# gMLP projections in two passes, with Strassen's algorithm for u and g

## The chip, the cores and the metric

The kernel runs on one core of a Trainium2 chip. The metric is the device time of one execution in microseconds: 1731.4 us is the median of three runs of the kernel before (1731.1 to 1732.46). The trace shown below is one more execution, recorded by the hardware profiler.

## The reference

One layer of a hybrid encoder, sequence 4096, width 1024, everything in float32. With `h = RMSNorm(x) * norm_gain * (1 + scale) + shift`:

```
q, k, v, g_attn, u, v_gm, g_gm = split(h @ w_in)        # 512,128,128,512,512,512,512 columns
A  = windowed_GQA(q, k, v) * silu(g_attn)               # 128-token blocks, +-128 tokens
vn = rms(v_gm in 8 groups of 64)                        # per token and group
sv = einsum('gts,bcsge->bctge', w_s, vn) + b_s          # mixing inside each 128-token chunk
M  = u * sv * silu(g_gm)
out = x + gate * (concat[A, M] @ w_out)
```

shift, scale and gate come from `silu(c) @ w_ada + b_ada`. The norm gain and scale are folded into the weights per input row (`gcol`), the shift into a bias row (`bias1`, `bias2`), and the token's 1/rms (`rstd`) is multiplied in when a product leaves PSUM.

## The kernel before

The sequence is 32 blocks of 128 tokens. Each float32 operand is split into a high and a low part of type float32r (`h = copy(x)`, `l = x - h`), and each product is three matmuls per 128-row slice (high by high, high by low, low by high), so a block's product with 512 columns over 1024 rows is 8 x 3 = 24 matmuls of 512 columns (`proj_ops`, one PSUM bank). The high parts are copied on ScalarE (ACT), the low parts subtracted on VectorE (DVE) or GpSimd (POOL).

The program has a start (the conditioning, the weights of q, k, v and g_attn, L286 on) and three phases.

- **Attention** (L782 on, `run_iter`): per block the products k/v, q and g, with the attention of a block three back between them at positions given by `TUNE`. The last iterations have no attention products of their own, and eight products of the next phase fill them (`TUNE["vm"]`, `main_f`): v and g of blocks 0 to 3. The attention half of `y` goes transposed to DRAM (`yT[b][0]`).
- **gMLP** (L796 on): per block three products with the weights of v, g and u (`w2["v"]`, `w2["g"]`, `w2["u"]`, all split and resident). The block's x is loaded transposed (`xraw`, two buffers), split once by `split2` (`xh`, `xl`, two buffers each) and used by all three. `gmlp_v` takes v out of PSUM, normalizes it per group (Square on ACT, reduce on DVE, a power on POOL at L83, a multiply on DVE) and splits it into `vh`, `vl`. Every four blocks `gmlp_mix` does the mixing (24 matmuls of 256 columns), multiplies `(sv + b_s)` into `u*g` on DVE, transposes the four blocks on TensorE (16 transposes) and sends them to `yT[b][1]`.
- **Output** (L1108 on): 16 pairs of blocks, each a 2 x 2 block product by Strassen's algorithm in Winograd's form: seven products of 12 matmuls (`prod3`, `ORDER`) into three PSUM banks X, Y and Z that are read between and added on (`post3`, `out3`). Its seven weight sets are sums of quarters of `gate * w_out`, built during the gMLP phase (`wo_rows`, `wo_sums`, `wo_last`), kept in DRAM (`wB`), loaded and split at the phase's start (`stage_w`, `split_wm`). Its operands are sums of quarters of a pair of blocks (`sum3` on POOL, `prep3` splits them).

Program order is that of the text, but the framework's scheduler orders each engine's queue by when it thinks an instruction is ready, earlier text first; instructions marked `keep_in_program_order` stay. On the chip each queue is in order. Loads and most stores are issued on SyncE's queue (SP), the stores of `yT[b][1]` on ACT's.

Of the kernel before, what the change touches and what calls it, by code (L numbers as in the profile page):

```python
# [42 lines left out]
def body(tc, x, xT, c, cT, w_adaT, b_adaT, w_gate, b_gate, ngT, w_in, q_gain, k_gain, sink, wsT, bsT, w_out, out):  # L43
# [591 lines left out]
    def sides1(i):  # L635
# [35 lines left out]
        if i == NB:  # L671
            add(TUNE["vx"], lambda: split_v(0))
            for m in range(KC // 2):
                add(TUNE["wv0"] + TUNE["wvd"] * m, lambda m=m: split_wf("v", m + 1))
        for m in range(KC // 2):
            pos = TUNE["wg0"] + TUNE["wgd"] * m
            if i == NB + int(pos):
                add(pos % 1, lambda m=m: split_wf("g", m + 1))
# [42 lines left out]
    c2 = {"u": 0, "v": DG, "g": 2 * DG}  # L721

    def halves(name):

        out = []
        for i, t in enumerate(("qf", "qf", "gf", "th", "qT", "qT", "gf", "ph", "pl", "ph", "pl", "ph", "pl", "ph")):
            n = {"qf": 2, "gf": 3, "th": 1, "qT": 2, "ph": 4, "pl": 4}[t]
            if t == "qT":
                q = base.tile([P, 2, 512], F32R, tag=t, name=f"{name}{i}", bufs=n)
                out += [q[:, 0], q[:, 1]]  # L730
            else:
                out.append(base.tile([P, 512], F32R, tag=t, name=f"{name}{i}", bufs=n))
        return out

    def alloc_w2(pool, n):
        if n == "u":
            ts = halves("w2u")
            w2[n] = ts[::2], ts[1::2]
        else:
            w2[n] = [[pool.tile([P, DG], F32R, tag=f"{t}{k}", name=f"w2{n}{t}{k}") for k in range(KC)] for t in "hl"]  # L740

    pending = [(n, k2) for n in "vgu" for k2 in range(KC // 2)]
    loaded = {}

    def load_w2():
        if not pending:
            return
        n, k2 = pending.pop(0)
        c0 = C1 + c2[n]
        name = f"w2raw{n}{k2}"  # L750
        if (n, k2) == ("v", 1):
# [449 lines left out]
```

## Time and profile before

| | before |
|---|---|
| median of three runs | 1731.4 us |
| the profiled execution | 1732.1 us |
| its span, first to last instruction | 1730.3 us |
| PE busy | 1661.7 us (96%) |
| DVE, ACT, POOL busy | 1075.7, 738.7, 689.4 us |
| granted TensorE clock, mean | 0.987 |
| HBM read, written | 128.5 MB, 40.9 MB |

A busy engine is one with an instruction in flight; PE is TensorE's matmuls, PEld its weight loads, which overlap them. Times are from the start of the span. The start lies at 0 to 100 us, attention to about 870 us (the filling products from about 785 us), gMLP to about 1400 us, output to the end.

### The profile page before, as it was taken

What the parts mean: (1) busy time and instruction counts of PE and PEld (TensorE: products, weight loads), DVE (VectorE), ACT (ScalarE), POOL (GpSimd) and SP (SyncE); (2) the same over time, 40 slices, a digit from 0 to 9 for tenths busy, and PEclk for the clock granted to TensorE, in tenths of its full rate; (3) what the DMA queues carried; (4) which work ended last, traced back from release to release, by engine and by line L of the source; (5) the groups of instructions that cost most, each with busy time, mean ns of one, the idle gap of its engine ahead of it and who ended that gap; (6) DMA issues with size and microseconds to landing.
All of it is one profiled execution on the core that took longest, in us unless ns stands there. A gap on an engine that the chain in (4) does not pass through costs nothing.

```text
span 1730.3 us, 23014 instructions
## 1 busy us (share of the span) xinstructions
PE 1661.7 (96%) x8216; PEld 1377.6 (80%) x8216; DVE 1075.7 (62%) x2279; ACT 738.7 (43%) x1613; POOL 689.4 (40%) x610
## 2 busy tenths in 40 slices
PE   6789999999999999998989999999999989999999
PEld 4578888888888888886778888887888877888887
DVE  7987777787777778779773333344443466444443
ACT  3476666666666666665421212211122233222221
POOL 5653343433344433336522222222222337545552
PEclk9899999999999999999999999999999999999999
DMA  7522112222112222122250111213233146555442
GB/s 257 195 86 74 57 54 74 74 74 74 48 63 74 73 74 80 35 70 79 75 183 30 49 37 49 84 69 116 104 116 97 56 166 216 165 164 180 150 149 83
DMA packets 67762, 170.92 MB, mean 99 GB/s; under 512 B 8256, under 2 KB 8256, under 8 KB 67648
## 3 DMA queue, kind: packets, MB, share of 16 engines
q1 hardware_dynamic: 62896, 160.81, 27.8%
q10 hardware_dynamic: 4752, 8.65, 1.3%
q8 instruction: 64, 1.05, 0.2%
q14 instruction: 50, 0.41, 0.1%
HBM read 128.54 MB, written 40.89 MB: 98 GB/s over the span
## 4 chain that ended last, share of the span: by engine, by line
PE 76%; DVE 11%; DMA 2%; ACT 2%; issue 1%; POOL 1%; SPq 0%; DVEq 0%; POOLq 0%; ACTq 0%
PE pg L61 16%; PE pv L61 9%; PE pq L61 9%; PE pu L61 8%; PE oY L967 7%; PE oZ L967 5%; PE oX L967 5%; PE s L61 4%; PE pT L64 4%; PE po L61 3%; DVE y L600 3%; DVE pr L551 1%; PE sv L61 1%; PE pk L61 1%; DVE gf L495 1%
## 5 line engine op out<-in xcount | busy, mean ns | idle before, releaser
L97 POOL TENSOR_TENSOR xl<-xraw,xh 128x1024 fp32r<-128x1024 f32 x58 | 149.8, 2582 | 366.7 <-ACT xh L96 366.7
L571 POOL TENSOR_SCALAR pr<-pr,den 128x384 f32<-128x384 f32 (+1 forms) x256 | 146.4, 591 | 162.4 <-DVE vs L445 119.0
L555 ACT ACTIVATE pr<-pr,mx 128x384 f32<-128x384 f32 (+1 forms) x256 | 153.8, 601 | 61.0 <-DVE mx L551 60.2
L551 DVE CUSTOM_DVE_ANT_0 pr<-s,negd,nsink 128x384 f32<-128x384 f32 (+1 forms) x256 | 152.5, 607 | 11.7 <-PE s L61 6.2
L580 ACT CAST ph<-pT 128x512 fp32r<-128x512 f32 x188 | 109.6, 584 | 115.7 <-PE po L61 43.0
L61 PE MATMUL pu<-w2u,xh 128*128 128x512 f32 x480 | 149.2, 392 | 0.0
L61 PE MATMUL s<-kT,qT 128*128 128x384 f32 (+1 forms) x512 | 136.4, 348 | 12.8 <-DVE mx L551 11.0
L581 DVE TENSOR_TENSOR pl<-pT,ph 128x512 fp32r<-128x512 f32 x188 | 126.0, 685 | 15.6 <-ACT ph L580 15.6
L83 POOL TENSOR_TENSOR ssv<-ssv,mhalf 128x8 f32<-128x8 f32 x32 | 54.3, 1696 | 183.3 <-DVE ssv L82 183.1
L64 PEld LDWEIGHTS pT<-ident,pr 128*128 128x128 f32 x752 | 93.3, 140 | 34.8 <-POOL pr L571 6.8
L64 PE MATMUL pT<-ident,pr 128*128 128x128 f32 x752 | 115.7, 274 | 5.2 <-DVE pl L581 3.5
L61 PEld LDWEIGHTS s<-kT,qT 128*128 128x128 f32 x512 | 87.3, 190 | 32.9 <-DVE mx L551 19.5
L61 PEld LDWEIGHTS pu<-w2u,xh 128*128 128x128 f32 x480 | 90.9, 189 | 18.8
L96 ACT CAST xh<-xraw 128x1024 fp32r<-128x1024 f32 x61 | 64.1, 1050 | 91.1 <-PE pu L61 89.0
L61 PE MATMUL pg<-wgh,xl 128*128 128x512 f32 x232 | 98.7, 425 | 0.0
L61 PE MATMUL pg<-wgh,xh 128*128 128x512 f32 x232 | 98.5, 424 | 0.0
L61 PE MATMUL pu<-w2u,xl 128*128 128x512 f32 x240 | 94.2, 392 | 1.2 <-DVE xl L97 1.2
L61 PE MATMUL pq<-w1h,xh 128*128 128x512 f32 x232 | 94.2, 406 | 0.0
L61 PE MATMUL pq<-w1l,xh 128*128 128x512 f32 x232 | 93.9, 405 | 0.0
L61 PE MATMUL pq<-w1h,xl 128*128 128x512 f32 x232 | 92.0, 396 | 0.0
L61 PE MATMUL pg<-wgl,xh 128*128 128x512 f32 x232 | 91.8, 396 | 0.0
L230 DVE SCALAR_TENSOR_TENSOR vf<-pv,rstd,bias 128x512 f32<-128x512 f32 x32 | 24.0, 750 | 108.9 <-PE pv L61 108.8
(337 smaller groups left out, 4511.4 us busy)
## 6 DMA issues: line engine op xcount, KB each, us to landing
xraw<-xT SPq DMA_DIRECT2D x61, 512.0 KB, 3.9
xtok<-x SPq DMA_DIRECT2D x32, 512.0 KB, 5.1
yr<-yT SPq DMA_DIRECT2D x64, 256.0 KB, 4.3
xt<-x SPq DMA_DIRECT2D x32, 512.0 KB, 3.8
out<-xt SPq DMA_DIRECT2D x64, 256.0 KB, 3.5
wada<-w_adaT SPq DMA_DIRECT2D x16, 512.0 KB, 5.7
yT<-ybuf ACTq DMA_DIRECT2D x32, 256.0 KB, 2.2
yT<-y SPq DMA_DIRECT2D x31, 256.0 KB, 5.2
```

Of the source, the lines that this page charges most:

```text
L61: pe(T.matmul(ps, lhsT, rhs, start=start, stop=stop))
L64: pe(T.transpose(ps, src, ident))
L83: G.tensor_tensor(dst, dst, mhalf[:, :width], ALU.pow)
L96: A.copy(xh, xr)
L97: ins = eng.tensor_tensor(xl, xr, xh.bitcast(F32), ALU.subtract)
L551: V.tensor_tensor_reduce(flat(t[:, s0:s1]), flat(pss[:, s0:s1]), flat(negd[:, b % 3, s0:s1]), -(2.0 ** -(h + 1)), nsink[:, h : h + 1], ALU ...
L555: A.activation(t, t, AF.Exp, bias=m[:, i : i + 1], scale=-1.0, accum_out=d["den", j][:, i : i + 1])
L571: G.tensor_scalar(t, t, den[:, i : i + 1], 1.0, ALU.mult, ALU.mult)
L580: A.copy(ph, pt)
L581: V.tensor_tensor(pl, pt, ph.bitcast(F32), ALU.subtract)
L600: V.tensor_tensor(d["y"][e * HD : (e + 1) * HD, 2 * j : 2 * j + 2], po[:HD, e::2], lo[:, e::2], ALU.add)
L967: pe(T.matmul(ps, l[:, k], r[k], start=i < 3 and k == 0 and j == 0, stop=k == KC // 2 - 1 and j == 2, skip_group_check=i >= 3))
```

## The change

The gMLP phase becomes two passes and the second shares its loop with the output phase.

- The attention's tail is filled with v of blocks 0 to 7 instead of v and g of blocks 0 to 3. Only the weights of v are split there; those of g and u are not kept as plain halves any more.
- **Pass A**: for blocks 8 to 31 only v is projected and normalized; a block's x is split in halves, low parts half on POOL and half on DVE. Every four blocks `mix` does the mixing, ACT adds `b_s` (8 activations with Identity) and 16 stores of 64 KB with 512-byte rows, on ACT's queue, keep sv in DRAM (`svB`). `rstd` is transposed once and kept in DRAM as a row (`rT`). The conditioning's gate moves to blocks 11 to 15; the Strassen weight sets of the u and g weights (as a 1024 x 1024 matrix) are built in blocks 16 to 27 and, for three sets, at the seam behind the pass.
- **Pass B**: u and g of a pair of blocks as one 2 x 2 block product in seven products of 12 matmuls. x is loaded again, multiplied by `rT` (broadcast to all partitions, one block on DVE, one on POOL), then `sum3` and `prep3` as in the output phase. `post_ug` adds biases, takes silu of g, multiplies sv and u; `tr_y` transposes the pair before and stores it.
- One loop of 32 pair steps: 0 to 15 are pass B, 16 to 31 the output product. In steps 15 and 16 the seven weight sets are replaced in place, each as soon as its last product with the old weights is done (14 loads of 512 KB through three buffers).

The core of the diff:

```diff
-TUNE = dict(... vm=[[], ["v0", "v1", "g0", "g1", "v2"], ["v3", "g2", "g3"]], ...
+TUNE = dict(... vm=[[], ["v0", "v1", "v2", "v3", "v4"], ["v5", "v6", "v7"]], ...
...
-        xs[b] = split_x(base, load_xT(base, b), b, V if nx[0] < 3 else G)
+        for i, eng in enumerate((G, V)):
+            k = slice(i * H, (i + 1) * H)
+            A.copy(xh[:, k], raw[:, k])
+            eng.tensor_tensor(xl[:, k], raw[:, k], xh[:, k].bitcast(F32), ALU.subtract)
...
+    def mix(b0):
...
+            sv = pb.tile([P, NC, 2, HD], F32, tag="sv", name=f"svt{b0}_{g2}", bufs=3)
+            for gi in range(2):
+                A.activation(sv[:, :, gi], ps[:, gi]..., AF.Identity, bias=bs[:, g : g + 1])
+            for c in range(NC):
+                nc.scalar.dma_start(svB[b0 + c][:, g2 * P : (g2 + 1) * P], sv[:, c]...)
...
+    def ug_direct(k, t):
+        A.activation(h, t[:, 0], AF.Copy, scale=gk)
+        V.scalar_tensor_tensor(l, t[:, 0], gk, h.bitcast(F32), ALU.mult, ALU.subtract)
+        G.tensor_scalar(t[:, 1], t[:, 1], gk, 1.0, ALU.mult, ALU.mult)
+        hl_w("B22", k, t[:, 1], G)
...
+    def norm3(p):
+        if p < NP:
+            for i, eng in enumerate((V, G)):
+                eng.tensor_tensor(r, r, gate[0][...]..., ALU.mult)
...
+    def post_ug(p, i):
+        if i == 0: V: p1 = X + bias_g
+        if i == 1: V: uB = Y + p1;  G: uB += bias_u - bias_g
+        if i == 3: V: gs1 = Y + p1; V: gs1 += Z;  A: silu(gs1);  G: gs1 *= sv1
+        if i == 4: V: uA = X + bias_u
+        if i == 5: V: gs0 = Y + p1;  A: silu(gs0);  G: gs0 *= sv0;  V: uA *= gs0
+        if i == 6: V: uB += Z;  V: uB *= gs1
...
+    for b in range(NF, NB):
+        if b + 1 < NB:
+            split2(b + 1)
+        proj2(b)
...
+        if b >= NF + NC and b % NC == 0:
+            mix(b - NC)
+        norm2(b)
+        if b >= NF + 2:
+            hl_v(b)
+        if 11 <= b < 15:
+            bg_gate(2 * (b - 11))
+            bg_gate(2 * (b - 11) + 1)
...
+        if 16 <= b < 28:
+            (ug_rows, ug_sums, ug_split)[(b - 16) % 3]((b - 16) // 3)
...
+    for p in range(2 * NP):
+        if p and p + 1 < 2 * NP:
...
+            norm3(p + 1)
+            sum3(p + 1, ("S1", "S2", "S3", "S4"))
...
+        for i in range(7):
+            prod3(p, i)
+            if i == 1 and 0 < p <= NP:
+                tr_y(p - 1)
+            (post_ug if p < NP else post_out)(p, i)
+            if i == 3 and p and p + 2 < 2 * NP:
+                load3(p + 2)
...
+            if p == 0 and i == 1:
+                for k in range(H):
...
+                    ug_direct(k, direct[k])
+                mix(NB - NC)
...
+                sum3(0, ("S3", "S4"))
...
+                for k in range(H):
+                    hl_w("T4", k, t4raw[k], G)
...
+            elif p + 1 < 2 * NP:
+                prep3(p + 1, i)
+            n = 7 * (p - NP + 1) + i - 2
+            if 0 <= n < 7:
+                for q in range(2):
+                    split_wm(SETS[n], q)
+                    if todo:
+                        stage_w(*todo.pop(0))
```

`post_ug` is told in short here: V, A and G are DVE, ACT and POOL. In pass A `sums3` of S3 and S4, the set T4 and the second pair of x buffers (`pc`) lie where `wsh`, `wsl`, `vh` and `vl` were (`pb`), and B21 and B22 where the weights of v were, so at step 0 they wait for the last mixing and the last v product.

## Rows read from the trace of the kernel before

**Rows 1.** The page's first part: busy time, share and count by engine.

```profile
PE 1661.7 (96%) x8216; PEld 1377.6 (80%) x8216; DVE 1075.7 (62%) x2279; ACT 738.7 (43%) x1613; POOL 689.4 (40%) x610
```

**Rows 2.** Stretches: length, busy us (count) by engine, clock, DMA share, GB/s.

```profile
976.65:1047.57 70.92, 70.92 (x329) 58.36 (x329) 23.74 (x40) 14.26 (x21) 17.97 (x8) 1.00 0.13 45
1460.00:1479.24 19.24, 19.24 (x86) 15.79 (x85) 8.43 (x13) 4.84 (x9) 10.24 (x7) 1.00 0.53 167
780.00:870.00 90.00, 80.27 (x374) 62.58 (x373) 76.08 (x153) 47.56 (x106) 51.53 (x51) 0.96 0.26 83
870.00:906.00 36.00, 30.21 (x136) 24.83 (x135) 28.41 (x29) 8.69 (x12) 7.63 (x3) 0.91 0.53 177
1405.60:1442.00 36.40, 27.69 (x112) 21.36 (x113) 20.89 (x27) 12.84 (x24) 21.00 (x14) 0.86 0.62 217
```

**Rows 3.** The chain that ended last, one block of gMLP: start, us, what.

```profile
1050.37 5.46 PE pg L61 x24
1055.83 5.44 PE pu L61 x24
1061.27 5.60 PE pv L61 x24
```

**Rows 4.** PE's timeline: first and last of twelve consecutive mixing matmuls.

```profile
1403.96 0.28 PE L61 MATMUL sv<-vh,wsh 128*128 128x256 f32 x1
...
1405.24 0.28 PE L61 MATMUL sv<-vh,wsl 128*128 128x256 f32 x1
```

**Rows 5.** Groups by line, 900 to 1250 us: count, busy us, mean ns, idle before.

```profile
L97 POOL TENSOR_TENSOR xl<-xraw,xh 128x1024 fp32r<-128x1024 f32 x19 | 53.3, 2805 | 136.2 <-ACT xh L96 136.2
L83 POOL TENSOR_TENSOR ssv<-ssv,mhalf 128x8 f32<-128x8 f32 x20 | 33.5, 1674 | 129.3 <-DVE ssv L82 129.3
L230 DVE SCALAR_TENSOR_TENSOR vf<-pv,rstd,bias 128x512 f32<-128x512 f32 x20 | 15.0, 751 | 80.5 <-PE pv L61 80.5
L247 DVE TENSOR_TENSOR vf<-vf,ssv 128x512 f32<-128x512 f32 x19 | 13.2, 692 | 32.8 <-POOL ssv L83 32.8
L243 ACT ACTIVATE sqv<-vf 128x512 f32<-128x512 f32 x20 | 12.6, 632 | 93.5 <-DVE vf L230 91.2 <-DMA yT<-ybuf 1.9 <-ACT ybuf L858 0.4
L818 ACT CAST vh<-vf 128x512 fp32r<-128x512 f32 x19 | 11.8, 621 | 73.5 <-DVE vf L247 73.5
```

**Rows 6.** Groups by line of ACT, the whole span.

```profile
L955 ACT CAST oA<-yr 128x512 fp32r<-128x512 f32 x32 | 19.8, 620 | 58.3 <-PE oZ L967 29.4 <-PE oX L967 28.3 <-DVE ssv L245 0.6
L419 ACT COPY bias<-start_pk 128x256 f32<-128x256 f32 x1 | 0.4, 372 | 0.8 <-PE start_pk L418 0.8
```

**Rows 7.** ACT's timeline: a store issued on ACT's queue, then its next copy.

```profile
1047.93 0.33 ACTq L859 DMA_DIRECT2D yT<-ybuf  x1
1048.49 0.59 ACT L858 COPY ybuf<-yT 128x512 f32<-128x512 f32 x1 [0.60 <-DMA yT<-ybuf]
```

**Rows 8.** Groups by line of POOL, the whole span: the sums of the output phase.

```profile
L949 POOL TENSOR_TENSOR s<-s,yr 128x512 f32<-128x512 f32 x16 | 27.6, 1723 | 1.2
L949 POOL TENSOR_TENSOR s<-yr 128x512 f32<-128x512 f32 x16 | 20.9, 1305 | 3.4 <-DMA yr<-yT 3.4
```

**Rows 9.** Groups by line of DVE, 780 to 906 us: splits of u's and g's weights.

```profile
L774 DVE TENSOR_SCALAR w2u<-w2rawu,gcol 128x512 fp32r<-128x512 f32 x4 | 5.7, 1440 | 0.5 <-PE po L61 0.5
...
L775 DVE SCALAR_TENSOR_TENSOR w2u<-w2rawu,gcol,w2u 128x512 fp32r<-128x512 f32 x4 | 3.7, 932 | 1.7 <-PE po L61 1.6
...
L775 DVE SCALAR_TENSOR_TENSOR w2gl<-w2rawg,gcol,w2gh 128x512 fp32r<-128x512 f32 x4 | 3.4, 849 | 0.0
L774 DVE TENSOR_SCALAR w2gh<-w2rawg,gcol 128x512 fp32r<-128x512 f32 x4 | 3.2, 815 | 0.0
```

**Rows 10.** The page's 40 slices of 43.3 us: DMA rate.

```profile
GB/s 257 195 86 74 57 54 74 74 74 74 48 63 74 73 74 80 35 70 79 75 183 30 49 37 49 84 69 116 104 116 97 56 166 216 165 164 180 150 149 83
```

**Rows 11.** DMA issues: queue, count, KB each, median us to landing.

```profile
xraw<-xT SPq DMA_DIRECT2D x61, 512.0 KB, 3.9
...
stT<-wB_T SPq DMA_DIRECT2D x8, 512.0 KB, 4.0
```

More of the change, by code (lines that the diff above doesn't have):

```diff
@@ L48, in body @@
     dram = ctx.enter_context(tc.tile_pool(name="dram", bufs=1, space=DRAM))
+    svB = [dram.tile([P, DG], F32, name=f"sv{b}") for b in range(NB)]
+    rT = dram.tile([1, S], F32, name="rT")
     yT = [[dram.tile([P, 4, P], F32, name=f"yT{b}_{h}") for h in range(2)] for b in range(NB)]
@@ L673, in sides1 @@
             for m in range(KC // 2):
[L674 to L678, printed above, removed]
+                add(TUNE["wv0"] + TUNE["wvd"] * m, lambda m=m: split_wf(m + 1))
         if i <= NB:
@@ L720, in body @@
     vr = None
[L721 to L742, printed above, removed]
+    pending = list(range(KC // 2))
     loaded = {}
@@ new lines, in body, with operand @@
+    H = KC // 2
+    NP = NB // 2
+    ORDER = (("A11", "B11", "X"), ("S2", "T2", "Y"), ("S3", "T3", "Z"), ("S1", "T1", "Y"), ("A12", "B21", "X"),
+             ("S4", "B22", "Y"), ("A22", "T4", "Z"))
+    SETS = tuple(m for _, m, _ in ORDER)
+    wts, staged, raw3, opnd, sums3, banks, E, chunk = {}, {}, {}, {}, {}, {}, {}, {}
+    gate = []
+    def operand(pool, n, tag, bufs):
+        o = pool.tile([P, 2, H, P], F32R, tag=tag, name=f"o{n}", bufs=bufs)
+        opnd[n] = o[:, 0], o[:, 1]
+    for n in ("A11", "S2"):
+        operand(pp, n, f"o{n}", 1)
@@ new lines, in body @@
+    for n in ("S1", "S2"):
+        sums3[n] = pp.tile([P, 512], F32, name=f"sum{n}")
+    ts = []
+    for i, t in enumerate(("qf", "qf", "gf", "th", "qT", "qT", "gf", "ph", "pl", "ph", "pl", "ph", "pl", "ph")):
+        n = {"qf": 2, "gf": 3, "th": 1, "qT": 2, "ph": 4, "pl": 4}[t]
+        if t == "qT":
+            q = base.tile([P, 2, 512], F32R, tag=t, name=f"wst{i}", bufs=n)
+            ts += [q[:, 0], q[:, 1]]
+        else:
+            ts.append(base.tile([P, 512], F32R, tag=t, name=f"wst{i}", bufs=n))
@@ L959, in prod3 @@
         n, m, z = ORDER[i]
-        if i == 0:
-            banks.update(
-                (z, pool.tile([P, 512], F32, tag=t, name=f"o{z}{p}")) for z, pool, t in (("X", ps_mm, "mm"), ("Y", ps_o, "o"), ("Z", ps_s, "s"))
-            )
-        ps, (xh, xl), (wh, wl) = banks[z], opnd[n], wts[m]
-        for k in range(KC // 2):
-            for j, (l, r) in enumerate(((xh, wh), (xh, wl), (xl, wh))):
-                pe(T.matmul(ps, l[:, k], r[k], start=i < 3 and k == 0 and j == 0, stop=k == KC // 2 - 1 and j == 2,
-                            skip_group_check=i >= 3))
@@ L970, in post3 @@
-    def post3(p, i):
-        p1, u2, u4 = part["p1"], part["u2"], ybuf[0]
+        if i < 3:
+            pool, t = {"X": (ps_mm, "mm"), "Y": (ps_o, "o"), "Z": (ps_s, "s")}[z]
+            banks[z] = pool.tile([P, 512], F32, tag=t, name=f"o{z}{p}")
+        ps, (xh, xl), (wh, wl) = banks[z], opnd[n], wts[m]
+        for k in range(H):
+            for j, (l, r) in enumerate(((xh, wh), (xh, wl), (xl, wh))):
+                pe(T.matmul(ps, l[:, k], r[k], start=i < 3 and k == 0 and j == 0, stop=k == H - 1 and j == 2,
+                            skip_group_check=i >= 3))
@@ L1158, in body @@
-    p3.close()
+    pbs = ExitStack()
+    pb = pbs.enter_context(tc.tile_pool(name="pb", bufs=1, reuse_waits="tile"))
+    wsh = pb.tile([P, NG, P], F32R, name="wsh")
+    wsl = pb.tile([P, NG, P], F32R, name="wsl")
+    bs = pb.tile([P, NG], F32, name="bs")
+    vh = pb.tile([P, NG, NC, HD], F32R, name="vh")
+    vl = pb.tile([P, NG, NC, HD], F32R, name="vl")
+    rrow = pb.tile([NB, P], F32, name="rrow")
+    split2(NF)
+    for b in range(NC):
+        norm2(b)
+        hl_v(b)
+    wsr = vr.tile([P, D], F32, tag="raw2", name="wsr", bufs=3)
```

515 lines of the change are left out of this document (235 added, 280 removed).

## The prediction

> **What bounds the kernel now.** I read the page's busy times first, then the chain that ended last, then stretches of each phase. PE is busy for 1661.7 of 1730.3 us, DVE for 62%, ACT and POOL for 43 and 40% [rows 1]. The chain through the gMLP phase is nothing but projections end to end: 24 matmuls of g in 5.46 us, of u in 5.44, of v in 5.60 [rows 3]. Twelve of them make 66.0 us, and a group of four blocks takes 70.92 us, in which PE is never idle; in the output phase the same holds for a pair of blocks, 19.24 of 19.24 us at the full clock [rows 2]. So in these two stretches time is the number of matmuls, and the other engines (DVE 23.7 of 70.9 us, ACT 14.3, POOL 18.0) set nothing. The remaining 4.9 us of a group are the mixing and the transposes: twelve mixing matmuls start within 1.28 us of each other, 0.116 us apart [rows 4], so 24 take 2.8 us and the 16 transposes 2.1, 0.13 each.
>
> PE loses time at two places. From 780 to 906 us, where attention runs out and gMLP starts, it is idle for 9.7 and 5.8 us, and the granted clock is 0.96 and 0.91, worth 0.04 x 90 + 0.09 x 36 = 6.8 us: 22 us in all [rows 2]. At the seam before the output loop (1405.6 to 1442 us) it is idle for 8.7 us and the clock is 0.86, 5.1 us more: 13.8 us [rows 2].
>
> **The change part by part.** The sum starts from the profiled execution's 1732.1 us, 1.8 above its span and 0.7 above the median of the runs.
>
> *Matmuls.* u and g of a pair of blocks are four products now, 2 x (5.46 + 5.44) = 21.80 us [rows 3]. As seven products of 12 they have the form of the output loop's pair, 19.24 us [rows 2]. 16 pairs x 2.56 = **-41.0 us**. The 32 products of v, the mixing and the 128 transposes stay. If all seven products ran at v's pace (5.60/24 = 0.233 us a matmul) a pair would be 19.6 us, at u's pace 19.0: +6 and -3 us over the pass.
>
> *Pass A.* A group of four blocks needs PE for 4 x 5.60 + 2.8 = 25.2 us. Beside it, for four blocks:
> - ACT: two half copies of x (0.62 each, as the output loop's copies of 512 columns [rows 6]), Square 0.63, the copy of v 0.62 [rows 5] = 2.5 a block, 10.0; eight additions of b_s on 256 columns from PSUM, 0.37 each by the nearest copy [rows 6] = 3.0; 16 stores, each 0.33 us of its queue [rows 7] = 5.3. Sum 18.3 us. In blocks 16 to 27 the new weight sets add, for three blocks, two scaled copies of 1024 columns (estimate 1.24 each, twice a 512) and four of 512: 5.0, or 6.6 for four: 24.9 of 25.2 us.
> - DVE: 0.75 out of PSUM and four operations at about 0.69 [rows 5], 14.0 us. In blocks 11 to 14 eight gate steps of 1024 columns come on top, estimate 1.5 each: 26 us, a little over.
> - POOL: half of 2.81 for the split and 1.67 for the power [rows 5], 12.3 us, and about 5.6 for weight sets.
>
> So no engine is slower than PE, but ACT has nothing to spare. Per block the critical hand-over is x: its buffer is freed by the product two before, leaving 5.60 us for two ACT copies and 1.40 us of POOL, 2.6 us. The risk is the burst behind the mixing: 8 x 0.37 + 16 x 0.33 = 8.3 us of ACT against PE's 2.8, with two PSUM banks between. Ends: 0, since PE has the next block's product to put between, and (8.3 - 2.8) x 8 = 44 us if it puts nothing there. The nearest row is today's group, where eight DVE operations hang on the same two banks and PE has no idle [rows 2]; so I take **+4** (half a us a group). What waits behind ACT's stores is the next copies of x, with 3 us of slack; an sv buffer is reused after three stores' rounds, which may hold ACT's fourth.
>
> *The filling products.* Eight before, eight after. DVE no longer splits the weights of u and g there: 5.7 + 3.7 + 3.4 + 3.2 = 16 us [rows 9] off an engine that is busy for 104 of 126 us [rows 2]; POOL and ACT lose their shares. Added are four more splits of x, two 0.62 us copies and 2.8 us of POOL each, every one needed by one product instead of two. Ends: -16 (all of DVE's work was in the way) and +8 (each split late by half of its 4 us). I take **-5**, nearer to nothing because attention's own DVE and ACT work stays.
>
> *Seam from pass A to B.* Replaces the seam that costs 13.8 us. The last v product is followed by 0.75 + 0.63 + 0.69 + 1.67 + 0.69 + 0.62 + 0.69 = 5.7 us [rows 5] until the mixing can run; the first two Strassen products (2 x 2.75, a seventh of 19.24 each) stand beside that. Then S3 must be summed where `wsh` lay, POOL 1.3 to 1.7 us [rows 8], and split, 1.3: 3 us, in part covered by the fourth product. POOL has about 28 us of work in the first 27 us of pass B (B22's four scalings and subtractions 9, T4 6, S3 and S4 3, the next pair's normalizing and sums 9), so a late B22 or T4 is possible. Loss 10 us with the clock's share, **-4** against today. Ends -10 and +8.
>
> *Pass B.* Per pair PE needs 19.24 + 8 x 0.13 = 20.3 us. POOL: 2.8 for normalizing a block, seven operations of 1.3 to 1.7 [rows 5, 8]: 12 to 15. DVE: 1.4, seven splits and nine operations at 0.69: 12.4. ACT: seven copies, two silu, two copies from PSUM, two stores: 7.4. All under 20.3. DVE does wait for POOL's multiplication by sv at the sixth product, with the next pair's preparation queued behind it, which has six products (16 us) of slack. **+1**; ends 0 and +16 (1 us a pair).
>
> *Seam from B to C.* No pause is planned: each of the seven weight sets is replaced behind its last use, five products ahead of its next. That is 14 loads of 512 KB, three of them earlier, so 5.8 MB in seven products (19 us), beside the loop's own traffic at 165 GB/s, 3.2 MB [rows 2]: 9.0 MB. The highest rate of a slice is 257 GB/s [rows 10], at which this takes 35 us; the last set is due 10 products, 27.5 us, after the first is freed. The sets alone take 23 us. One load lands in 4.0 us [rows 11] and three buffers are in turn. POOL's half of the splitting adds 2 x 1.5 us to its 1.4 in each slot of 2.75 us, 31 us for seven, 3 us late. **+4**, ends 0 and +10; the kernel's end is unchanged.
>
> The Trainium skill (DMA: Bandwidth & Descriptors, Specifications) puts a core's HBM limit at about 358 GB/s. At that, 9.0 MB take 25 us, the sets come in time and the sum would be 4 us lower; no stretch shown here goes over 257.
>
> Sum: 1732.1 - 41.0 + 4 - 5 - 4 + 1 + 4 = 1691.1, and 0.7 less for the median: **1690.4 us**.
>
> **The rivals.**
> 1. *ACT keeps x back (slower).* If ACT's queue has a block's copy of v ahead of the copies of x for the block two further on, x follows the whole chain: 0.75 + 0.63 + 0.69 + 1.67 + 0.69 + 0.62 = 5.05 us, then 0.62 + 1.40, with eight hand-overs about 7.6 us a block instead of 5.60. 24 x 2.0 = 48 us in place of the 4: 1735, slower. It decides from 41/24 = 1.7 us a block on. For it: that is the order of the text. Against: the queues are ordered by readiness, and x is ready five us earlier; today's phase never shows it, but it has three products per x. 7%.
> 2. *The burst holds PE* for its whole 5.5 us a group: 1690 + 40 = 1730, no change. Against it stands the group without idle time [rows 2]. 4%.
> 3. *Pass B isn't bound by PE:* POOL's and DVE's hand-overs make a pair 22 us, nothing is gained by fewer matmuls: 1730. Against it, 15 us of POOL and 12 of DVE in 20. 4%.
> 4. *Both seams are bad:* POOL's 28 us of work arrive late at step 0 (+8 instead of -4) and the weights at step 16 (+10 instead of +4): 1708. For it: traffic of 217 GB/s at today's seam goes with its waits [rows 2]. 14%.
> 5. *The fill is freed entirely* (-16) and the seam costs 4 us (-10): 1673. For it: DVE is the busiest engine beside PE there [rows 2]. 11%.
>
> **How the numbers follow.** The forecast, 1680 to 1702, has 60%. The range leaves out the slow rivals and the far half of rival 5: **1675 to 1713**. A measurement of this kernel can tell 0.2% (3.5 us) from no change. Faster: the forecast, rivals 4 and 5, 85%; same: most of rivals 2 and 3, 6%; slower: rival 1 and what of 2 and 3 goes past it, 9%.
>
> **What would show it.** PE's count down by 192 matmuls; a pair of pass B at 20.3 us without idle, else rival 3. In pass A 25.2 us for four blocks; idle PE before v's product, released by POOL's or DVE's low part of x, with ACT's copy starting late, is rival 1, idle before mixing matmuls released by ACT is rival 2. From 780 to 906 us less idle time. At step 0 PE waiting for S3, B22 or T4, at step 16 for a split weight. I am wrong if PE idles regularly within a group or a pair, or if the output loop's pairs leave 19.24 us.

## The result: slower, 1823.6 us

The changed kernel takes 1823.64 us (median of four runs, 1822.72 to 1824.83) beside 1731.84 for the kernel before (median of four, 1731.10 to 1732.46): a ratio of 1.053, 95% interval 1.051 to 1.055. Predicted were 1690.4 us and a range of 1675 to 1713.

### The profile page after: what moved, and what is told of

It reads as the page before. It is cut to its first block, busy times and chain, and to the rows that moved or that the text cites. A ratio compares the mean times of both kernels' runs of the same rounds, so it can differ in the third digit from the quotient of the medians.

```text
span 1823.1 us, 23772 instructions
## 1 busy us (share of the span) xinstructions
PE 1654.0 (91%) x8025; PEld 1355.6 (74%) x8025; DVE 1229.6 (67%) x2414; ACT 848.2 (47%) x1838; POOL 890.6 (49%) x754
## 5 line engine op out<-in xcount | busy, mean ns | idle before, releaser
L969 ACT CAST oS<-sumS 128x512 fp32r<-128x512 f32 x128 | 79.5, 622 | 247.2 <-PE oY L980 169.6
L970 DVE TENSOR_TENSOR oS<-sumS,oS 128x512 fp32r<-128x512 f32 x128 | 114.6, 896 | 57.0 <-ACT oS L969 56.8
L100 POOL TENSOR_TENSOR xl<-xraw,xh 128x1024 fp32r<-128x1024 f32 x30 | 71.9, 2397 | 166.2 <-ACT xh L99 166.2
L64 PE MATMUL s<-kT,qT 128*128 128x384 f32 (+1 forms) x512 | 136.7, 348 | 16.8 <-DVE mx L537 15.8
L969 ACT CAST oA<-r 128x512 fp32r<-128x512 f32 x96 | 59.4, 620 | 136.8 <-PE oX L980 85.8
L64 PEld LDWEIGHTS s<-kT,qT 128*128 128x128 f32 x512 | 87.8, 191 | 37.2 <-DVE mx L537 24.2
L980 PE MATMUL oY<-wB22h,oS 128*128 128x512 f32 x256 | 90.5, 415 | 18.9 <-DVE e_gs L1004 16.9
L980 PE MATMUL oZ<-wst,oS 128*128 128x512 f32 x384 | 100.8, 414 | 6.5 <-ACT oS L969 6.5
L64 PE MATMUL pg<-wgh,xh 128*128 128x512 f32 x232 | 98.2, 423 | 0.0
L970 DVE TENSOR_TENSOR oA<-r,oA 128x512 fp32r<-128x512 f32 x96 | 77.5, 807 | 29.3 <-ACT oA L969 29.2
L980 PE MATMUL oY<-wst,oS 128*128 128x512 f32 x384 | 93.0, 390 | 3.6 <-DVE e_uB L999 3.5
L980 PE MATMUL oY<-wT2h,oS 128*128 128x512 f32 x256 | 87.5, 403 | 9.6 <-ACT oS L969 9.6
```

What stands on the lines that cost most here:

```text
L64: pe(T.matmul(ps, lhsT, rhs, start=start, stop=stop))
L100: ins = eng.tensor_tensor(xl, xr, xh.bitcast(F32), ALU.subtract)
L969: A.copy(flat(h), src)
L970: V.tensor_tensor(flat(l), src, flat(h).bitcast(F32), ALU.subtract)
L980: pe(T.matmul(ps, l[:, k], r[k], start=i < 3 and k == 0 and j == 0, stop=k == H - 1 and j == 2, skip_group_check=i >= 3))
```

## The profile after

The page's first part, to be held against [rows 1], and its rows of slices for PE, its granted clock and the DMA rate [rows 10]:

```profile
PE 1654.0 (91%) x8025; PEld 1355.6 (74%) x8025; DVE 1229.6 (67%) x2414; ACT 848.2 (47%) x1838; POOL 890.6 (49%) x754
...
PE   6799999999999999987877796789889988999999
...
PEclk9899999999999999998989898899999999999999
...
GB/s 260 181 70 70 70 70 70 70 70 70 70 65 57 58 77 59 63 82 139 96 119 109 132 108 100 151 138 128 144 129 162 121 159 214 171 139 181 165 139 81
```

The matmuls did go: 8216 to 8025, 191 fewer. PE's busy time fell by 7.7 us all the same, not by 41, and PE is now idle for 169 us of the span instead of 69. The slices say where: from the 18th to the 34th, PE has sixes, sevens and eights in thirteen of 17, where the kernel before had nines in nearly all, and the clock drops with them.

The stretches of the trace, in the columns of [rows 2]: fill, pass A (first product of block 8 to first of pair 0), one group of four blocks in it, pairs 0 and 1, pairs 2 to 14, one quiet pair, the seam B to C (pairs 15 and 16), the rest:

```profile
783.60:874.80 91.20, 76.09 (x346) 58.91 (x347) 72.11 (x141) 42.32 (x98) 47.77 (x40) 0.93 0.33 111
874.80:1095.80 221.00, 174.56 (x750) 139.23 (x749) 125.48 (x176) 100.42 (x188) 95.96 (x62) 0.91 0.37 114
990.70:1028.50 37.80, 27.63 (x122) 22.15 (x121) 21.61 (x31) 17.61 (x32) 17.49 (x12) 0.91 0.37 112
1095.80:1175.30 79.50, 51.71 (x202) 40.13 (x201) 56.76 (x55) 24.89 (x45) 58.24 (x35) 0.81 0.39 122
1175.30:1471.40 296.10, 273.66 (x1197) 219.94 (x1196) 187.91 (x239) 86.62 (x144) 162.78 (x104) 0.97 0.42 136
1245.90:1266.90 21.00, 20.55 (x94) 16.60 (x93) 12.96 (x17) 6.81 (x12) 12.94 (x9) 1.00 0.34 109
1471.40:1527.40 56.00, 44.63 (x185) 34.77 (x184) 40.53 (x45) 27.27 (x49) 40.40 (x29) 0.94 0.62 200
1527.40:1822.00 294.60, 291.98 (x1261) 236.21 (x1259) 123.59 (x190) 69.02 (x114) 144.18 (x99) 1.00 0.46 151
```

By the terms of the prediction:

| stretch | PE's own work | predicted loss | measured | beyond it |
|---|---|---|---|---|
| pass A, 24 blocks and 7 mixings | 24 x 5.6 + 7 x 2.8 = 154 | 4 | 221.0 | 63 |
| pairs 0 and 1, one mixing | 2 x 20.3 + 2.8 = 43.4 | 10 | 79.5 | 26 |
| pairs 2 to 14 | 13 x 20.3 = 263.9 | 1 | 296.1 | 31 |
| pairs 15 and 16 | 20.3 + 19.24 = 39.5 | 4 | 56.0 | 12 |

These make 133 us, all of the miss. The fill adds 13 (attention's last output product ends at 875.0 us, 866.7 before, 5 earlier forecast). The two are more than the miss because the forecast let 17 of the 22 us lost there stand, and 9 of the 22 (5.8 idle, 0.09 x 36 of clock [rows 2]) lay behind 870 us, in what is now the stretch of pass A, where the table allows nothing for them; 4 us are left over. In no stretch is another engine full: in pass A DVE is busy for 57% and ACT for 45%. So it is waits. PE's, in pass A (the matmul that waited, its line, what it waited for, us in total, times, longest; sv is the mixing, pv the product of v):

```profile
PE sv L64 <- ACT vh L815: 27.2, 5, 8.1
PE pv L64 <- ACT xh L797: 11.0, 4, 6.1
PE sv L64 <- DVE vl L816: 6.3, 4, 2.8
PE pv L64 <- POOL xl L798: 1.7, 3, 0.6
```

The longest one, engine by engine. Block 19's product ends at 990.9, that of block 20 at 996.5, and the mixing of blocks 16 to 19 is next in PE's queue. DVE's timeline, then POOL's, ACT's and PE's:

```profile
994.81 0.75 DVE L235 SCALAR_TENSOR_TENSOR vf<-pv,rstd,bias 128x512 f32<-128x512 f32 x1
...
996.53 1.75 DVE L798 TENSOR_TENSOR xl<-xraw,xh 128x512 fp32r<-128x512 f32 x1
998.20 0.67 DVE L241 TENSOR_REDUCE ssv<-sqv 128x8 f32<-128x512 f32 x1
998.80 1.15 DVE L878 TENSOR_TENSOR ugraw<-ugraw,ugraw 128x512 f32<-128x512 f32 x1
...
1002.15 1.74 DVE L243 TENSOR_TENSOR vf<-vf,ssv 128x512 f32<-128x512 f32 x1 [1.53 <-POOL ssv L86]
```

```profile
1000.11 2.01 POOL L86 TENSOR_TENSOR ssv<-ssv,mhalf 128x8 f32<-128x8 f32 x1 [0.71 <-DVE ssv L85]
```

```profile
1003.93 0.62 ACT L815 CAST vh<-vf 128x512 fp32r<-128x512 f32 x1 [3.32 <-DVE vf L243]
```

```profile
995.83 0.40 PE L64 MATMUL pv<-w2vl,xh 128*128 128x512 f32 x1
996.07 0.39 PE L64 MATMUL pv<-w2vh,xl 128*128 128x512 f32 x1
1004.60 0.80 PE L64 MATMUL sv<-vh,wsh 128*128 128x256 f32 x2 [8.14 <-ACT vh L815]
1005.19 0.63 PE L64 MATMUL pv<-w2vh,xh 128*128 128x512 f32 x1
1005.62 0.63 PE L64 MATMUL pv<-w2vl,xh 128*128 128x512 f32 x1
```

The chain that the prediction summed to 5.7 us takes 13.7, though no operation in it is long. The product's way out of PSUM starts 3.9 us late, behind other work in DVE's queue; the reduction stands behind the split of x; the product of vf, 0.69 in [rows 5], takes 1.74. And when PE comes back, its matmuls of 512 columns start 0.43 us apart in place of 0.24: after 8.1 us without a matmul the granted clock is 0.50 from 1004.6 to 1008.0 us, the lower of its two levels (1.2 in place of 2.4 GHz).

Then ACT's part: eight additions of b_s and 16 stores issued from its queue (the group over pass A; ACT's timeline behind the same mixing, a row being several of a kind; svt is the tile in which ACT leaves sv for the store):

```profile
L828 ACT ACTIVATE svt<-sv,bs 128x256 f32<-128x256 f32 x56 | 24.4, 473 | 48.1 <-issue 21.1 <-DMA sv<-svt 20.3 <-PE sv L64 6.7
```

```profile
1013.34 2.37 ACTq L830 DMA_DIRECT2D sv<-svt  x4
1015.76 0.48 ACT L828 ACTIVATE svt<-sv,bs 128x256 f32<-128x256 f32 x1 [1.98 <-issue]
...
1016.26 1.77 ACTq L830 DMA_DIRECT2D sv<-svt  x4
1020.15 0.62 ACT L815 CAST vh<-vf 128x512 fp32r<-128x512 f32 x1 [3.40 <-DVE vf L243]
...
1021.21 2.17 ACT L797 CAST xh<-xraw 128x512 fp32r<-128x512 f32 x4
```

Four stores take 1.8 to 2.4 us of the queue, not 1.3. The burst lasts from 1007.4 to 1018.0 us, and the copies of x come behind it and behind a copy of v that is not ready: 1021.2.

## The experiments

Each is read by its stretches (us; pairs 0 to 2 are taken together, since later kernels interleave them). PE's own work would be 154, 63.7, 243.6 and 39.5. Experiments 1 to 14 ran once each. Run again, the kernel of experiment 13 differs by at most 2.0 us in a stretch (47.6 for pairs 15 and 16), and eleven runs of it lie between 1723.2 and 1728.4: smaller differences than these are no evidence. The fill, written the same in all of them, ends between 873.5 and 877.8 us.

| kernel | pass A | pairs 0-2 | pairs 3-14 | pairs 15, 16 | time |
|---|---|---|---|---|---|
| changed | 221.0 | 101.2 | 274.4 | 56.0 | 1823.6 |
| 1 stores on SP | 195.1 | 98.4 | 277.3 | 55.8 | 1799.2 |
| 2 one store per tile | 205.7 | 100.1 | 285.7 | 57.3 | 1819.8 |
| 3 mixing later | 216.7 | 99.5 | 274.2 | 55.2 | 1817.3 |
| 4 = 2 + 3 | 183.4 | 100.1 | 287.0 | 55.6 | 1799.3 |
| 5 = 1 + 3 | 179.8 | 99.4 | 275.1 | 56.4 | 1782.2 |
| 6 = 5, subtractions on DVE | 170.5 | 100.2 | 277.4 | 56.1 | 1779.2 |
| 7 w_out later | 221.8 | 98.2 | 261.0 | 55.1 | 1808.6 |
| 8 POOL relieved in pass B | 219.7 | 97.6 | 279.0 | 55.6 | 1825.8 |
| 9 = 6 + 7, five svt | 170.0 | 96.3 | 265.2 | 55.5 | 1759.1 |
| 10 = 9, memory at the seam | 168.7 | 86.9 | 261.1 | 56.1 | 1747.8 |
| 11 half the staging bytes | 219.9 | 100.7 | 274.6 | 54.6 | 1822.8 |
| 12 = 10, POOL off the seams | 169.2 | 86.0 | 265.3 | 48.5 | 1742.2 |
| 13 = 12, norm behind u | 168.6 | 83.7 | 250.0 | 49.6 | 1726.7 |
| 14 = 13 with POOL's work back | 168.6 | 85.0 | 256.7 | 52.1 | 1738.2 |
| 15 = 13, four stores a mixing | 169.2 | 78.9 | 249.8 | 48.2 | 1721.3 |

**Pass A (1 to 6).** Experiment 1:

```diff
-                nc.scalar.dma_start(svB[b0 + c][...], sv[:, c]...)
+                nc.sync.dma_start(svB[b0 + c][...], sv[:, c]...)
```

> The 16 stores of each mixing go into SP's queue instead of ACT's; nothing else changes. Stretch read: the 24 products of pass A, 874.8 to 1095.8 us in the changed kernel, 221.0 us, about 64 us over 24 x 6.3 + mixing. Theory ACT (the stores, 0.3 to 0.7 us each in ACT's in-order queue, hold back the copies of x and of v behind them): 16 x 0.45 = 7.2 us come off ACT at each of 6 mixings; pass A falls to 180-195 us, the kernel to 1785-1800. Theory chain (the mixing is queued in PE straight behind its last product and waits for evacuation, norm and the copy of v, 13.7 us long, with DVE's and POOL's queues ahead): the wait on the copy stays, pass A stays at 210-221, the kernel at 1812-1824.

Measured: 195.1 and 1799.2, at the slow end of the theory ACT; PE's waits for vh fall from 27.2 to 16.8 us, those for xh from 11.0 to 2.8. (Over 24 x 6.3 us and seven mixings of 2.8 the changed kernel's excess would be 50 us, not the 64 named; by the table's 5.6 a block it is 67.) Experiment 2 keeps them on ACT and makes them four:

```diff
-            for c in range(NC):
-                nc.scalar.dma_start(svB[b0 + c][...], sv[:, c]...)
+            nc.scalar.dma_start(svB[b0 // NC][:, :, ...], sv.rearrange("p c a e -> p c (a e)"))
```

> One DRAM tile for four blocks, so that a mixing issues 4 stores in place of 16, still on ACT. Theory ACT: 12 x 0.45 = 5.4 us off each mixing's burst; pass A 185-200 us in place of 221.0, kernel 1790-1802. Theory chain: 210-221 and 1812-1824. If this gains and the stores on SP don't, it is the number of transfers and not ACT's issue.

Measured: 205.7, between the two theories; the time hardly moved, since pairs 3 to 14 grew by 11 us. Why they did is open: 4 shows it too (287.0), 15, which has this edit on SP, does not (249.8). Experiment 3:

```diff
         proj2(b)
...
-        norm2(b)
-        if b >= NF + 2:
-            hl_v(b)
+        else:
+            post2(b - 1)
```

where `post2` is mixing, norm and copy of v as they stood.

> Norm, copy of v and mixing of a block are written one block later (behind the next block's product), so that PE has a product of 6.3 us between the last product of a group and its mixing, and stands 13.7 us chain against 6.3 + 6.3. Stores stay on ACT. Theory chain: most of the 8.1 us wait at each of 5 mixings goes, pass A falls by 30-40 us to 180-190, kernel 1783-1793. Theory ACT: the copies of x still wait behind the burst of 10.7 us, pass A stays over 205, kernel over 1808.

Measured: 216.7, and PE's waits for vh fell only from 27.2 to 12.8 us: the chain alone is not it.

> Both: mixing one block later and 4 stores per mixing. If the two causes are separate their gains add: 30-40 from the chain and 20-30 from the stores, pass A 155-170 us, kernel 1760-1775. If each alone suffices to starve PE, this gains much more than the sum of the two alone. If neither is the cause (DVE and POOL slowing each other), pass A stays over 200.

> The two edits that stretch pass A: norm, copy of v and mixing one block later, and the 16 stores in SP's queue (SP has no wait for a store of its own to finish before ACT's next, which the variant with one store per tile had: PE waited 6.8 us for a tile of svt). Pass A (first product of block 8 to first product of pair 0; 221.0 in the changed kernel, 195.4 with the stores on SP, 215.9 with the mixing later, 183.9 with the mixing later and one store a tile). Theory 'either of ACT's burst and the chain is enough to starve PE': 165-180 us, kernel 1770-1785. Theory 'DVE and POOL are the floor (130 and 97 us busy of 184, with DVE's two-input operations at 1.75 in place of 0.68 us beside POOL's)': 180-195, kernel 1785-1800.

Measured: 183.4 and 179.8. The later mixing is worth 4 us by itself, 15 with the stores off ACT and 22 with four of them: where only one of the two causes is taken away, the other still stops PE. What then was left, 26 us over PE's own work, experiment 6 puts to DVE and POOL:

```diff
-        for i, eng in enumerate((G, V)):
+        for i, eng in enumerate((V, V)):
...
-        hl_w("B11", k, ra[:, 0], G)
+        hl_w("B11", k, ra[:, 0], V)
...
```

and the same for T1 and T3.

> As the kernel with both, and POOL's subtractions of pass A (the low half of xl, the low parts of the weight sets) done by DVE. DVE gets 23 + 12 operations of 0.68 us more (24 us), POOL loses as many of 1.3 to 1.7 us. Theory contention (a two-input operation of DVE waits for POOL's, 0.68 becomes 1.75): DVE's busy time in pass A does not rise, or falls, and pass A is 5-20 us shorter than without this edit. Theory no contention (the long ones are long for another reason): DVE's busy time rises by 24 us and pass A grows or stays.

The stretch of pass A in experiment 5, then three groups of DVE in it; and the same of experiment 6:

```profile
874.00:1053.80 179.80, 164.18 (x750) 132.76 (x749) 126.98 (x175) 95.60 (x184) 91.01 (x61) 0.95 0.44 137
```

```profile
L243 DVE TENSOR_TENSOR vf<-vf,ssv 128x512 f32<-128x512 f32 x23 | 25.6, 1111 | 40.9 <-POOL ssv L86 40.9
L798 DVE TENSOR_TENSOR xl<-xraw,xh 128x512 fp32r<-128x512 f32 x23 | 24.2, 1054 | 3.0 <-ACT xh L797 2.9
...
L241 DVE TENSOR_REDUCE ssv<-sqv 128x8 f32<-128x512 f32 x24 | 16.3, 678 | 1.8 <-ACT sqv L239 1.7
```

```profile
877.50:1048.00 170.50, 161.09 (x750) 129.97 (x749) 119.74 (x209) 96.06 (x184) 44.09 (x27) 0.98 0.46 144
```

```profile
L798 DVE TENSOR_TENSOR xl<-xraw,xh 128x512 fp32r<-128x512 f32 x46 | 29.7, 683 | 0.2 <-ACT xh L797 0.2
...
L241 DVE TENSOR_REDUCE ssv<-sqv 128x8 f32<-128x512 f32 x24 | 16.3, 679 | 1.8 <-ACT sqv L239 1.7
L243 DVE TENSOR_TENSOR vf<-vf,ssv 128x512 f32<-128x512 f32 x23 | 15.9, 692 | 41.8 <-POOL ssv L86 41.8
```

DVE does 34 operations more in 7.2 us less: its own fell from 1054 to 683 ns and from 1111 to 692 once POOL's subtractions were gone. What POOL took over had cost DVE as much in waiting as doing it. The Trainium skill (SBUF — State Buffer, Who interferes with whom) states this: a VectorE instruction with two SBUF inputs contends with a GpSimd one that reads SBUF, and one with at most one SBUF input, outside the modes that use both ports, does not. The traces agree, also in what is spared: the reduction, with one input, takes 0.68 us in both. The kernel gained 3.0 us of pass A's 9.3: its fill ended 3.5 later, and pass B took 3.

**Pairs 3 to 14 (7, 12 to 14).** In pair 3 of the changed kernel DVE has the multiplication of a row of w_out by the gate at the head of its queue, 5.4 us before its load lands; e_gs, which frees PE's bank, is behind it (DVE's and PE's timelines):

```profile
1214.53 1.23 DVE L909 TENSOR_TENSOR woraw<-woraw,gate 128x1024 f32<-128x1024 f32 x1 [5.38 <-DMA woraw<-w_out]
...
1216.40 0.68 DVE L1004 TENSOR_TENSOR e_gs<-oY,e_p 128x512 f32<-128x512 f32 x1
```

```profile
1217.23 0.77 PE L980 MATMUL oY<-wB22h,oS 128*128 128x512 f32 x1 [4.81 <-DVE e_gs L1004]
```

```diff
-            V.tensor_mul(flat(t), flat(t), gate[0][:, :D])       # wo_rows, pair p
+        with tc.issue_after(E["mark"].ins):                      # wo_sums, pair p + 1, behind uA
+            for t in (ra, rb):
+                V.tensor_mul(flat(t), flat(t), gate[0][:, :D])
```

> The changed kernel with one edit in pass B: the multiplications of w_out's rows by the gate stand on DVE a pair later, behind u's sum of that pair, so that DVE does not stand at the head of its queue for a load that has just been issued. Pairs 1, 3, 6 and 9 take 35.2, 28.6, 28.3 and 27.6 us beside 20.3. Theory 'w_out's load at the head of DVE's queue': pairs 3, 6 and 9 fall to 20.3-22, the pairs with the work (2, 5, 8, 11) stay under 23, kernel 1797-1805. Theory 'the DVE work itself, 5.2 us in one pair': the excess only moves to the other pairs, kernel 1815-1825.

Measured: pairs 3, 6 and 9 at 23.1, 23.1 and 24.1, the others of pairs 3 to 14 at 20.3 to 22.9, and 1808.6: between the theories, with 13 us of the 31. What of the rest is w_out's work and what another wait, this run does not tell; experiment 13 does. In experiment 8 T4 and the norms go to DVE alone:

```diff
-                    hl_w("T4", k, t4raw[k], G)
+                    hl_w("T4", k, t4raw[k], V)
...
-            for i, eng in enumerate((V, G)):
+            for i, eng in enumerate((V, V)):
```

> The changed kernel with POOL relieved in pass B: both halves of the norm of x and the low parts of T4 on DVE. At the seam A to B pairs 0 and 1 take 44.2 and 35.2 us beside 20.3. Theory 'POOL's queue is the seam' (T4 4 x 1.7, norms 2.9 to 3.4, sums 4 x 1.3 to 1.7 and the products with sv follow each other on POOL without a gap): pairs 0 and 1 together lose 8-15 us, kernel 1808-1816. Theory 'the mixing of the last blocks and the reload of x behind it are the seam': under 4 us, kernel 1819-1825; other pairs stay at 20.3 in both.

Measured: 3.6 us less in pairs 0 to 2, 4.6 more in the next twelve, where DVE still had w_out's waits; 1825.8. PE's wait of 9.0 us for u in pair 0 falls to 2.7, those for S2 and S3 (9.6 and 6.5) only to 7.8 and 6.4. So the norms and T4 alone are not the seam; the sums and B22 stayed on POOL.

**The seams (9 to 12).** Experiment 9 adds up what gained and gives the last two svt tiles other memory:

```diff
+            if g2 >= 2 and b0 < NB - NC:
+                sv = sums3[f"S{g2 - 1}"].rearrange("p (c a e) -> p c a e", c=NC, a=2)
```

> Adds up the edits that gained: mixing one block later, its stores on SP, POOL's subtractions of pass A on DVE, the multiplications of w_out a pair later; and the last two of the four svt tiles of a mixing are other memory, so that ACT doesn't wait for a store to land (PE waited 7.5 us for svt). If the causes are separate and in separate passes: 1779.2 - 15.2 (w_out) - 4 to 7 (svt) = 1757-1760, pass A 163-167 us. If w_out's gain was only time that the next stall would have taken anyway, over 1765.

Measured: 1759.1, within the forecast, but pass A stayed at 170.0: the svt tiles gained nothing, and 3.2 us of the gain are a fill that ended earlier. Experiment 10:

```diff
+    for n, t in (("S3", "h4"), ("S4", "h5")):
+        sums3[n] = vr.tile([P, 512], F32, tag=t, name=f"sum{n}")
+    raw3[1] = [vr.tile([P, KC, P], F32, tag=f"lp{i}", ...) for i in range(2)]
+    sum3(0, ("S3", "S4"))
...
-            if p == 0 and i == 1:
+            if p == 0 and i == 3:
...
                 mix(NB - NC)
...
-        G.tensor_scalar(t[:, 1], t[:, 1], gk, 1.0, ALU.mult, ALU.mult)
-        hl_w("B22", k, t[:, 1], G)
+        A.activation(t[:, 1], t[:, 1], AF.Copy, scale=gk)
```

> As the kernel with all of these, and the seam A to B taken apart: the x of pair 1 and the sums S3 and S4 lie in memory that is free with the last product of pass A (the low parts of w2v) in place of that of the mixing, and the mixing of the last four blocks stands behind four products of pair 0 in place of two. Pairs 0 and 1 took 78 us beside 2 x 20.3. Theory 'the seam is that pair 0's S3 and pair 1's x wait for the last mixing to free memory': the two fall to 44-55 us and the kernel to 1728-1736. Theory 'it is the load on POOL, DVE and ACT, whatever the order (weights T4 and B22, two norms, two sets of sums)': over 65 us, kernel over 1745.

Measured: pairs 0 and 1 at 67, outside the 44 to 55 of the first theory and in the second. The three stretches fell by 9 us, but the edit also takes POOL's work on B22 (scaling to ACT, low parts to DVE) and half of its T4 away, so how much of the 9 us is memory is open. PE's longest waits at the seam of the changed kernel, and POOL's timeline before the first of them:

```profile
PE oY L980 <- ACT oS L969: 9.6, 1, 9.6
PE yT L67 <- DVE e_uA L1012: 9.0, 1, 9.0
PE oZ L980 <- ACT oS L969: 6.5, 1, 6.5
```

```profile
1098.62 2.79 POOL L952 TENSOR_TENSOR r<-r,gate 128x1024 f32<-128x1024 f32 x1
1101.36 1.71 POOL L855 TENSOR_TENSOR wB22l<-ugraw,wB22h 128x512 fp32r<-128x512 f32 x1
...
1106.38 1.26 POOL L963 TENSOR_TENSOR sumS<-sumS,r 128x512 f32<-128x512 f32 x1
```

The first is for S2, whose sum stands behind the norm, B22's subtractions and S1 in POOL's queue. The second is for u of pair 0: POOL multiplies its factor behind the sums of pair 1, whose x SP loads only at 1124.1, after 19.1 us of waiting for the memory of svt. The third is for S3: its sum waits 2.6 us for the last mixing's matmuls, and its copy on ACT, at 1126.2, stands behind the mixing's stores (1116.4 to 1125.1); with the stores on SP (experiment 9) this wait is 1.5. Experiment 11:

```diff
-        nc.sync.dma_start(t, wB[m][:, 2 * i : 2 * i + 2])
+        nc.sync.dma_start(t[:, 0], wB[m][:, 2 * i])
```

> The changed kernel with half the bytes of the weights of pass C loaded (each staging load brings one of its two rows of 512, which is used for both; the output product is then not the reference's). The last pair of pass B and the first of pass C take 24.7 and 31.3 us beside 20.3 and 19.45, and 7 sets of 1 MB are loaded in them. Theory 'the loads are the seam': 41-46 us for the two, kernel 1810-1814. Theory 'the splitting of the weights (28 copies and 28 subtractions on ACT, DVE and POOL beside u and y of the last pair)': over 51 us, kernel 1818-1824.

Measured: 54.6 and 1822.8. Half the bytes (each load brings one of its two rows and lands in 3.0 us in place of 5.3) change nothing clear of the scatter: my forecast's reason for that seam, DMA rate, is refuted. Experiment 12 takes POOL out of both seams:

```diff
-            hl_w(m, 2 * i + j, t[:, j], (V, G)[j])
+            hl_w(m, 2 * i + j, t[:, j], V)
...
-            G.tensor_tensor(sums3[n], q[a], q[b], op)
+            (G if p else V).tensor_tensor(sums3[n], q[a], q[b], op)
```

and the norms of pairs 0 and 1, the rest of T4 and gs0's product with sv to DVE.

> As the kernel with the seam taken apart (1747.8 us), and POOL's part in three places on DVE: norm of x and sums of pair 0, norm of pair 1 and T4's low parts at the seam A to B; the product of gs0 with sv in every pair of pass B; the low parts of the second row of each weight chunk of pass C. Theory 'POOL's in-order queue and its slowing of DVE hold both seams': pairs 0 and 1 fall from 67 to 48-58 us, pairs 15 and 16 from 26.7 + 29.4 to 42-49, the pairs between (mean 21.5) to 20.6-21.2, kernel 1718-1732. Theory 'DVE is then the bound': the pairs between grow over 22 and the kernel stays over 1742. Where only one of the three gains, its stretch shows which.

Measured: B to C falls by 7.6 to 48.5, with two things moved there, the splitting and gs0's product; A to B stays at 86.0, and pairs 3 to 14 go to 22.1 in the mean, which the second theory would call DVE as the bound. The trace of this kernel says otherwise (DVE's and PE's timelines): for 5.3 us DVE does nothing, with the next pair's norm at its head and u behind it.

```profile
1356.16 1.22 DVE L959 TENSOR_TENSOR r<-r,gate 128x1024 f32<-128x1024 f32 x1 [5.33 <-DMA r<-xT]
1357.31 0.68 DVE L1020 TENSOR_TENSOR e_uA<-e_uA,e_gs 128x512 f32<-128x512 f32 x1
```

```profile
1358.13 0.63 PE L67 MATMUL yT<-ident,e_uA 128*128 128x128 f32 x4 [3.00 <-DVE e_uA L1020]
```

```diff
-            norm3(p + 1)
+                with tc.issue_after(E["last"].ins):
+                    norm3(p + 1)
...
-            if i == 3 and p and p + 2 < 2 * NP:
+            if i == (0 if p + 2 < NP else 3) and p and p + 2 < 2 * NP:
                 load3(p + 2)
```

> As the kernel with POOL's work of the seams moved (1742.2 us), and DVE's order in pass B: the norm of x for pair p+1 stands behind the last product of u in pair p-1, and its load is issued three products earlier; the two multiplications of w_out stand apart, behind uB and gs1 of their pair. Pairs 3 to 14 of pass B took 22.1 us in the mean. Theory 'a load's wait at the head of DVE's queue holds u, and with it y's transposes in PE's queue': 20.3-20.9 in the mean, kernel 1722-1730. Theory 'DVE is the bound with POOL's work on it': over 21.7, kernel over 1738.

> The same order of DVE, with POOL's norms, sums and products left on POOL as in the kernel of 1747.8 us, except for the low parts of pass C's weights, which DVE makes. If the order of DVE's queue is what counts in pass B: pairs 3 to 14 at 20.3-20.9, pairs 0 and 1 as before (67 us), pairs 15 and 16 under 49, kernel 1722-1732. If POOL's part slows DVE: pairs over 21.3 and the kernel 1735-1742.

Measured: 1726.7 and 1738.2. Pairs 3 to 14 take 20.8 us, eight of them 20.3 and the four with w_out's work 21.8 to 22.0: a wait at the head of DVE's queue, not DVE's load. The edit changes the order and issues the load of x earlier; which of the two counts more was not tried. With POOL's work back they take 21.4: 6.7 us over the twelve, though DVE has less to do. In these pairs the only work that goes back is gs0's product. The seam B to C takes 52.1 with it, beside 49.6 and 47.6 in the two runs of 13 and 48.5 in 12: of the 56.1 of experiment 10 the splitting is worth about 4 and gs0's product about 3, if DVE's new order counts for nothing there.

**The best version.** With the stores on SP, a wait that was left at the seam A to B sat in SP's queue; SP's timeline of experiment 13, then of 15, which issues 4 stores per mixing:

```profile
1033.64 5.22 SPq L836 DMA_DIRECT2D sv<-svt  x8
1039.16 3.74 SPq L836 DMA_DIRECT2D sv<-sumS  x8
1043.01 3.23 SPq L949 DMA_DIRECT2D r<-xT  x3
```

```profile
1034.47 1.25 SPq L835 DMA_DIRECT2D sv<-svt  x2
1038.41 0.33 SPq L948 DMA_DIRECT2D r<-xT  x1
```

> As the kernel of 1726.7 us with 4 stores per mixing in place of 16 on SP (one DRAM tile for four blocks). The load of the second x of pair 0 was issued at 1043.0, when SP had issued the 16 stores of the mixing before it (1033.6 to 1042.5), and PE waited 5.3 us for S2. Theory 'SP's queue': that load is issued before 1040 and the wait falls under 2 us; pairs 0 and 1 lose 4-8 us, kernel 1718-1724. Theory 'the norm of blocks 30 and 31 at the head of DVE's queue': the wait stays, kernel 1725-1728. Pass A stays at 166-171 us: with five svt tiles the store's landing no longer matters as it did with three on ACT's queue (pass A 204).

> The kernel of 1726.7 us again, timed in rounds against the kernel before: 1724.5-1728, 0.2 to 0.4% under 1731.8, interval under 1.

Measured: 1721.28 us, ratio to the kernel before 0.9937 (0.9918 to 0.9955), and for experiment 13 again 1725.41, 0.9966 (0.9954 to 0.9978). x is loaded 4.6 us earlier, PE's wait of 5.3 us for S2 is gone and pairs 0 to 2 lose 4.8. So the algorithm is worth 0.6% when its queues are in order and POOL is out of DVE's way, and costs 5.3% when they are not: the difference, 102 us, is waits and their clock, since both have 8025 matmuls.

## Why the prediction was wrong

- *Matmuls, -41:* right. 191 fewer, and an undisturbed pair of pass B takes 20.3 us, as forecast. Pairs of pass C take 19.45 in place of 19.24.
- *Pass A, +4:* this step failed, by 63 us. I priced the burst of ACT at 8.3 us, with 3 us of slack for the copies of x behind it, and bounded it at 44, then took the value of a row of the old kernel, where the same two banks were emptied by DVE and three products stood behind each x. The burst is 10.7 us. The chain into the mixing, which one product was to cover, is 5.7 us as a sum of durations and 13.7 in the trace, because each engine's queue puts other work between. Rival 1 (7%) is seen: the copies of x stand behind a copy of v that is not ready, and PE waits 12.7 us for x. Of rival 2 (4%) only the sign came: PE's waits before the mixing are released by ACT, but by its copy of v; none names the additions that empty the banks. Experiments 1, 3 and 5 show that burst and chain each stop PE without the other; 9 us more are DVE and POOL slowing each other (experiment 6), which the sum did not have: its rows came from a kernel with POOL at 18 of 70.9 us [rows 2].
- *The clock:* not in pass A's sum. The same 750 matmuls of pass A are 174.6 us of PE's time at a granted 0.91 and 159.7 at 0.99 in experiment 13: about 15 of the 63 us are the lower level, which came eight times in pass A, each time behind one of PE's longer waits.
- *Seam A to B, 10 us:* 36. S3, B22 and T4 were named, and POOL's 28 us of work; the price was too low. Three waits of PE make 25 us of it: for S2 (9.6) behind B22 in POOL's queue, for u of pair 0 (9.0), of which experiment 8 leaves 2.7, and for S3 (6.5) behind the last mixing and its stores. Experiment 10 gained 9 us by memory and by less work on POOL together. The 5 us of experiment 15 belong to stores on SP, which the changed kernel has on ACT. 15 us over PE's work remain there (78.9 against 63.7).
- *Pass B, +1:* 32. The sum for DVE left out the rows of w_out altogether. More than their work, their loads' wait at the head of DVE's queue cost it (13 us, experiment 7), and then the norm's (15 more, experiment 13, which also sets w_out's two multiplications apart). Rival 3 (4%) had the size, 22 us a pair, but not these waits.
- *Seam B to C, +4:* 16.5, and for another reason: half the bytes changed nothing, and PE's waits there, 11.4 us, all name DVE's work on u, g and the output, none a weight. POOL's half of the splitting is about 4 of it and its product of gs0 about 3; the rest is open. Rival 4 (14%) had both seams bad, but at 22 (13.8 + 8) and 10 us.
- *Fill, -5:* +8. PE waits 9.1 us in it for DVE's maximum of attention's scores, 4.4 in the kernel before. Why was not tried.

## What to carry to other kernels

A chain across four engines is not the sum of its durations: add for each engine what its in-order queue may hold ahead, and above all an operation that waits for a load or for another engine. Before giving an engine the other half of a job, look at what each does to the other's operations: with POOL on the other half, DVE's half of the subtractions of x took 24.2 us, and the whole without POOL 29.7. And where a change removes PE's work, the slack that this work gave to the hand-overs goes with it, and the chance of slower should follow that slack: here three products per x became one.

## Not expected of the hardware

DVE's two-input operations of 512 columns took 0.68 us alone and 1.75, at most 2.9, beside one of POOL, while its one-input reduction stayed at 0.67. A store of 64 KB on ACT's queue held it for 0.33 to 0.72 us, four of the 128 for 1.3 to 1.8. Halving 7 MB of loads in a stretch of 56 us at 200 GB/s moved it by 1.4, less than two runs of one kernel differ there (2.0).
